# A transformer layer on one core: weight halves and matmul operands placed at chosen remainders of 128 bytes

## The chip, the cores and the metric

The kernel runs on one core of a Trainium2 chip. A core has a matrix engine (TensorE, PE in the rows; its weight loads are shown apart as PEld), a vector engine (VectorE, DVE), an activation engine (ScalarE, ACT), GpSimd (POOL) and a queue engine (SyncE, SP) that issues the transfers. The core's own memory has 128 partitions; a tile takes the same stretch of bytes in each of them, so that an address below is a byte offset within a partition. The metric is the device time of one execution in microseconds, median of several runs.

## The reference

One layer with 512 tokens and model width 2048, all in float32. Cut to what matters here:

```python
mod = silu(c) @ w_ada + b_ada                       # six vectors of 2048
h = rms_norm(x, norm1_g) * (1 + sc1) + sh1
proj = h @ w_in                                     # 2048 x 7168
o_hg = hgrn2_mixer(...)                             # 8 heads of gated recurrence
o_sb = stick_breaking_mixer(...)                    # 8 heads of causal attention
x = x + g1 * (concatenate([o_hg, o_sb]) @ w_out)    # 2048 x 2048
h = rms_norm(x, norm2_g) * (1 + sc2) + sh2
gate, up = split(h @ w_ffn_in)                      # 2048 x 11264
x = x + g2 * ((silu(gate) * up) @ w_ffn_out)        # 5632 x 2048
```

## The kernel before, in words

TensorE runs its big products at full rate in a reduced float32 format. To keep float32 accuracy each operand is split into a high half and a low half, and each product is three matmuls: high by high, high by low, low by high (`three`, `product`, `multiply`). The activations are split once and stay in memory (hhi and hlo, later ohi and olo, then opA to opD, then opsA to opsC). The weights are streamed: a transfer brings a tile into the ring "raw" (four buffers), `split` (L214) writes the high half with ScalarE (L220) and the low half with VectorE (L221) into the ring of three "hi" and three "lo" buffers of 4096 bytes, and TensorE reads those. From the input loop on, every fourth split goes to a pair of spare tiles instead: in the input loop hi2 and lo2 from the pool tp (`spare_here`, L1096), in the output half a part of the tile opsB (`spare_there`, from L1154).

The stages follow each other: the first projection (16 steps, accumulators st), eight heads of attention projection (sbp) with the attention of earlier heads between them, three projections per recurrence head (hgf, hgq, hgg) with the recurrence between them, the output projection (wo), a first gate tile (ff), the input loop of the feed-forward part (tiles f = 2 to 43; 7 products of 24 matmuls each, by a Strassen-like scheme, into ffA, ffB, ffC), and the output half (foA, foB, foC; 12 units of 7 products). VectorE also forms the rows of w_ada times c (L180) between them. The order of instructions is fixed when the program is built, by the code and by a planned clock in `Clock`; at run time each engine goes through its list in order.

In the first projection, in the attention projection and in the output half, a split weight tile is the moving operand and an activation tile the stationary one (in a row of a matmul, the names behind the arrow are the moving operand and then the stationary one). In the recurrence heads, the output projection and the input loop it is the other way round. Within a tile every slice that a matmul reads begins at a multiple of 512 bytes from the tile's start.

Where a tile starts is set by the pools. Left-hand pools stack from the low end in the order in which they are opened: const (cond, small, ones, epsb, lead, mod, gain1, gain2, rcol, ident2 and others), wp (raw, hi, lo), hp, and the stage's pools; a pool with side="right" stacks down from the top. Each tile is rounded up to 32 bytes. The small tiles of const (epsb of 4 bytes, lead of 8, rcol of 16) therefore set the remainder of everything behind them.

| tile | start before | remainder by 128 |
|---|---|---|
| ring raw | 11040 | 32 |
| ring hi (3 x 4096), ring lo | 43808, 56096 | 32 |
| hhi, ohi, opB, opsC | 68384 | 32 |
| hlo, olo, opC, opsB | 101152 | 32 |
| opA, opsA | 133920 | 32 |
| opD | 166688 | 32 |
| xo, x1, O | 196576 | 96 |
| spare hi2, lo2 of the input loop | 213984, 218080 | 96 |
| spare of the output half | within opsB | 32 |

Of the kernel before, what the change touches and what calls it, by code (L numbers as in the profile page):

```python
# [10 lines left out]
F32 = mybir.dt.float32  # L11
F32R = mybir.dt.float32r
# [5 lines left out]
P = 128  # L18
# [17 lines left out]
EPS = 1e-6  # L36
# [93 lines left out]
def trunk(ctx, tc, a):  # L130
    nc = tc.nc
    V, S, G = nc.vector, nc.scalar, nc.gpsimd
# [2 lines left out]

    const = ctx.enter_context(tc.tile_pool(name="const", bufs=1))
    wp = ctx.enter_context(tc.tile_pool(name="wp", bufs=3))
    xctx = ctx.enter_context(ExitStack())
    xop = xctx.enter_context(tc.tile_pool(name="xop", bufs=1, side="right"))
    hp = ctx.enter_context(tc.tile_pool(name="hp", bufs=1))  # L140
# [14 lines left out]
    ones = const.tile([P, P], F32, name="ones")  # L155
    G.memset(ones, 1.0)
    one = ones[:, 0:1]
    epsb = const.tile([P, 1], F32, name="epsb")
    G.memset(epsb, EPS)
    lead = const.tile([P, 2], F32, name="lead")  # L160
    left = [KT] * 6
    mod = const.tile([P, 96], F32, name="mod")
    gain1 = const.tile([P, KT], F32, name="gain1")
    gain2 = const.tile([P, KT], F32, name="gain2")
    rcol = const.tile([P, 4], F32, name="rcol")
    ident2 = const.tile([P, P], F32, name="ident2")

    def small_col(base, i=0):
        return small[:, base + i:base + i + 1]
# [9 lines left out]
    def gemv(w, row, col):  # L179
        V.scalar_tensor_tensor(w, w, 1.0, row, op0=ALU.mult, op1=ALU.mult, accum_out=col)  # L180

    def finish_gain(comp, k0, k1):
        g, base = (gain1, C_N1) if comp == SC1 else (gain2, C_N2)
        V.scalar_tensor_tensor(g[:, k0:k1], mod[:, comp * KT + k0:comp * KT + k1], 1.0, small[:, base + k0:base + k1],
                               op0=ALU.add, op1=ALU.mult)

    def ada(comp, k):
        j = comp * KT + k
        c = slice(j, j + 1)
        gemv(row_load(a["w_ada"][j], f"ada{j}"), cond, mod[:, c])  # L190
        left[comp] -= 1
        if comp == SC1:
            V.tensor_add(mod[:, c], mod[:, c], small_col(C_BADA, j))
            finish_gain(comp, k, k + 1)
        elif not left[comp]:
            all_k = slice(comp * KT, comp * KT + KT)
            V.tensor_add(mod[:, all_k], mod[:, all_k], small[:, C_BADA + comp * KT:C_BADA + comp * KT + KT])
            if comp == SC2:
                finish_gain(comp, 0, KT)
# [12 lines left out]
    def split(r, shape, name):  # L212
        count[0] += 1
        if spare and count[0] % 4 == 0:  # L214
            hi, lo = spare[0](shape, name)
        else:
            hi = wp.tile(shape, F32R, tag="hi", name=name + "h")
            lo = wp.tile(shape, F32R, tag="lo", name=name + "l")
        with tc.high_priority(offset=AHEAD):
            S.copy(hi, r)  # L220
            V.tensor_sub(lo, r, hi.bitcast(F32))  # L221
        return hi, lo

    def weights(src, shape, name):
        return split(load(src, shape, name), shape, name)
# [60 lines left out]
    for k in range(KT):  # L286
        xk = xo[:, k]
        if k == 0:
            for i in range(2):
                sl = slice(i * 1024, i * 1024 + 1024)  # L290
                gemv(r0[:, sl], cond[:, sl], lead[:, i:i + 1])
            j = SC1 * KT
            V.scalar_tensor_tensor(mod[:, j:j + 1], lead[:, 0:1], lead[:, 1:2], small_col(C_BADA, j), op0=ALU.add, op1=ALU.add)
            finish_gain(SC1, 0, 1)
            whi = wp.tile([P, 1024], F32R, tag="hi", name="wi0h")
            wlo = wp.tile([P, 1024], F32R, tag="lo", name="wi0l")
            for sl in (slice(0, T), slice(T, 2 * T)):
                S.copy(whi[:, sl], w0[:, sl])
                V.tensor_sub(wlo[:, sl], w0[:, sl], whi[:, sl].bitcast(F32))
        else:  # L300
            nc.sync.dma_start(xk, a["x"][:, k])
            ada(SC1, k)
            if k == 2:
                nc.sync.dma_start(cst, a["cst"])
            if k == KT - 1:
                nc.sync.dma_start(ident2, a["cst"][:, 0])
            whi, wlo = weights(a["w_hi"][k], [P, 1024], f"wi{k}")
        gk = gain1[:, k:k + 1]
        S.activation(hhi[:, k], xk, AF.Identity, scale=gk)
        V.scalar_tensor_tensor(hlo[:, k], xk, gk, hhi[:, k].bitcast(F32), op0=ALU.mult, op1=ALU.subtract)  # L310
        if k == 0:
            S.activation(ss1, xk, AF.Square)
        else:
            sq = sb.tile([P, T], F32, tag="qT" if k % 2 else "kT", name=f"sq{k}", bufs=1)
            S.activation(sq, xk, AF.Square)
            V.tensor_add(ss1, ss1, sq)
        for n in range(2):
            for t in range(4):
                ts_ = slice(t * P, t * P + P)
                cs = slice(n * T, n * T + T)  # L320
                out = banks[n * 4 + t]
                PE.matmul(out, hhi[:, k, ts_], whi[:, cs], start=(k == 0), stop=False)
                PE.matmul(out, hhi[:, k, ts_], wlo[:, cs], start=False, stop=False)
                PE.matmul(out, hlo[:, k, ts_], whi[:, cs], start=False, stop=(k == KT - 1))
# [12 lines left out]
    def sb_project(h):  # L337
        ps = [acc(f"sbp{h}_{t}") for t in range(4)]
        for c in range(8):
            if c % 2 == 0:  # L340
                raw = load(a["w_sb"][h, c // 2], [P, 2, 2, 384], f"wsb{h}_{c}")
            whi, wlo = split(raw[:, c % 2], [P, 2, 384], f"wsb{h}_{c}")
            pairs = [(kk, t) for kk in range(2) for t in range(4)]
            if c in (0, 7):
                pairs.sort(key=lambda p: p[1])
            for kk, t in pairs:
                k = 2 * c + kk
                ts_ = slice(t * P, t * P + P)
                out = ps[t][:, 0:384]
                PE.matmul(out, hhi[:, k, ts_], whi[:, kk], start=(k == 0), stop=False)  # L350
                PE.matmul(out, hhi[:, k, ts_], wlo[:, kk], start=False, stop=False)
                PE.matmul(out, hlo[:, k, ts_], whi[:, kk], start=False, stop=(k == KT - 1))
                clock.run()
        clock.until(lambda: h not in reuse or reuse[h] in done)
        if h in (0, 3):
            rows = scr[:, 0:3].rearrange("p a b -> p (a b)").rearrange("p (t c) -> p t c", t=4)
        else:
            rows = sb.tile([P, 4, 384], F32, tag="rows", name=f"rows{h}")
        for t in range(4):
            if t % 2:  # L360
                V.tensor_copy(rows[:, t], ps[t][:, 0:384])
            else:
                S.copy(rows[:, t], ps[t][:, 0:384])
        ready[h] = rows
# [234 lines left out]
    def mtile(src, name, xhi, xlo, out, nk=KT):  # L599
        n = 0  # L600
        raw = load(src, [P, nk, P], name)
        for c0 in range(0, nk, HALF):
            w = min(HALF, nk - c0)
            whi, wlo = split(raw[:, c0:c0 + w], [P, w, P], f"{name}_{c0}")
            for kk in range(w):
                three(out, whi[:, kk], wlo[:, kk], xhi[:, c0 + kk], xlo[:, c0 + kk], n == 0, n == nk - 1)
                n += 1
                clock.run()
# [734 lines left out]
```

## Time and profile before

| | |
|---|---|
| median of 3 runs | 2309.77 us (2309.41 to 2312.48) |
| the profiled execution's own time | 2309.45 us |
| its span, first to last instruction | 2307.6 us |
| mean granted TensorE clock | 0.995 of full |
| TensorE, VectorE, ScalarE busy | 2253.1, 1919.5, 1160.1 us |

The page gives busy times and their share of the span; a matmul's own duration there overlaps its neighbours', so the distance between the starts of two matmuls tells more than the duration of one. A window row gives, for a stretch in microseconds from the span's start, its length, the busy time of each engine with the number of instructions, the granted clock as a share of full, the transfers' share and their GB/s. A row of the chain of waits merges consecutive pieces of the same line and engine: start, length, what, and how many.

### The profile page before, as it was taken

How to read it: one execution, taken by the hardware profiler on the slowest of the kernel's cores; microseconds unless marked ns; L12 is line 12 of the kernel's file. 1: busy time of each engine (PE TensorE's matmuls, PEld its weight loads, DVE VectorE, ACT ScalarE, POOL GpSimd, SP SyncE). 2: the span in 40 equal slices, each digit the busy share in tenths (PEclk: the TensorE clock that was granted, in tenths of full speed). 3: DMA queues.
4: the chain of work that ended last, by engine and by line, in shares of the span. 5: the costliest groups of instructions: out<-in, count | busy, mean ns of one | idle time of the engine just before them, and what ended most of it. 6: DMA issues, size and time to landing. Idle time of an engine off the chain costs nothing.

```text
span 2307.6 us, 35720 instructions
## 1 busy us (share of the span) xinstructions
PE 2253.1 (98%) x14171; PEld 2049.8 (89%) x14171; DVE 1919.5 (83%) x2570; ACT 1160.1 (50%) x2011; POOL 10.7 (0%) x25
## 2 busy tenths in 40 slices
PE   8999899999999999989999999999999999999998
PEld 6899799888888788989999999999999978878776
DVE  8887779999887864699899988888888777888888
ACT  4326666565656422654445444454545545454443
POOL 0000000000000000000000000000000000000000
PEclk9999999999999999999999999999999999999999
DMA  9886446843322486336555534454544486654553
GB/s 368 314 319 225 166 153 230 305 170 126 110 92 76 155 294 209 111 114 238 206 203 197 209 133 165 142 174 142 174 142 157 177 343 237 219 178 142 183 204 87
DMA packets 114978, 437.69 MB, mean 190 GB/s; under 512 B 9822, under 2 KB 58236, under 8 KB 76796
## 3 DMA queue, kind: packets, MB, share of 16 engines
q1 hardware_dynamic: 114812, 435.42, 53.0%
q8 instruction: 111, 1.82, 0.3%
q14 instruction: 55, 0.45, 0.1%
HBM read 386.61 MB, written 48.77 MB: 189 GB/s over the span
## 4 chain that ended last, share of the span: by engine, by line
PE 79%; DVE 11%; DMA 4%; ACT 3%; issue 3%; SPq 0%; DVEq 0%; ACTq 0%
PE ffA L93 17%; PE ffC L93 9%; PE foA L93 8%; PE sbp L93 8%; PE wo L93 7%; PE ffB L93 4%; PE foC L93 4%; PE st L93 4%; PE hgf L93 4%; PE hgq L93 3%; PE hgg L93 3%; PE foB L93 1%; DVE ada L180 1%; PE l L93 1%; DMA opd<-fhi 1%
## 5 line engine op out<-in xcount | busy, mean ns | idle before, releaser
L180 DVE SCALAR_TENSOR_TENSOR ada<-ada,cond 128x2048 f32<-128x2048 f32 x95 | 216.9, 2286 | 49.0 <-DMA ada<-in_w_ada 49.0
L93 PE MATMUL ffA<-opD,ff_3h 128*128 128x256 f32 x512 | 93.6, 283 | 0.8 <-ACT u L1008 0.8
L93 PE MATMUL ffA<-opB,ff_6h 128*128 128x256 f32 x512 | 93.6, 283 | 0.2 <-ACT a L1008 0.2
L93 PE MATMUL ffC<-opB,ff_7h 128*128 128x256 f32 x512 | 93.5, 283 | 0.0
L93 PE MATMUL ffC<-opC,ff_4h 128*128 128x256 f32 x496 | 90.8, 284 | 0.4 <-ACT c L1008 0.3
L93 PE MATMUL ffB<-opA,ff_2h 128*128 128x256 f32 x496 | 91.3, 284 | 0.0
L93 PE MATMUL ffA<-opC,ff_5h 128*128 128x256 f32 x496 | 90.6, 283 | 0.0
L93 PE MATMUL ffA<-opA,ff_1h 128*128 128x256 f32 x496 | 90.6, 283 | 0.0
L1082 ACT CAST fhi<-forms 128x512 fp32r<-128x512 f32 (+1 forms) x63 | 43.6, 692 | 90.6 <-DMA opd<-fhi 74.1
L93 PEld LDWEIGHTS ffA<-opD,ff_3h 128*128 128x128 f32 x512 | 79.8, 192 | 1.0 <-ACT u L1008 1.0
L93 PEld LDWEIGHTS ffA<-opB,ff_6h 128*128 128x128 f32 x512 | 79.7, 192 | 0.4 <-ACT a L1008 0.4
L93 PEld LDWEIGHTS ffC<-opB,ff_7h 128*128 128x128 f32 x512 | 79.8, 192 | 0.0
L93 PEld LDWEIGHTS ffC<-opC,ff_4h 128*128 128x128 f32 x496 | 77.2, 192 | 0.8 <-ACT c L1008 0.8
L93 PEld LDWEIGHTS ffB<-opA,ff_2h 128*128 128x128 f32 x496 | 77.7, 193 | 0.1
L93 PEld LDWEIGHTS ffA<-opC,ff_5h 128*128 128x128 f32 x496 | 77.3, 192 | 0.0
L93 PEld LDWEIGHTS ffA<-opA,ff_1h 128*128 128x128 f32 x496 | 77.3, 192 | 0.0
L1083 DVE TENSOR_TENSOR forms<-forms,fhi 128x512 fp32r<-128x512 f32 (+1 forms) x63 | 49.0, 778 | 31.0 <-ACT fhi L1082 30.6
L93 PE MATMUL ffA<-opD,ff_3l 128*128 128x256 f32 x256 | 72.5, 283 | 0.0
L93 PE MATMUL ffC<-opB,ff_7l 128*128 128x256 f32 x256 | 72.4, 283 | 0.0
L93 PE MATMUL ffA<-opB,ff_6l 128*128 128x256 f32 x256 | 72.4, 283 | 0.0
L93 PE MATMUL ffB<-opA,ff_2l 128*128 128x256 f32 x248 | 70.3, 284 | 0.0
L93 PE MATMUL ffA<-opA,ff_1l 128*128 128x256 f32 x248 | 70.2, 283 | 0.0
(1644 smaller groups left out, 7759.3 us busy)
## 6 DMA issues: line engine op xcount, KB each, us to landing
ada<-in_w_ada SPq DMA_DIRECT2D x95, 1024.0 KB, 5.0
wfo<-in_w_fo SPq DMA_DIRECT2D x16, 1024.0 KB, 6.0
yraw<-in_w_fo SPq DMA_DIRECT2D x16, 1024.0 KB, 5.1
fix<-in_w_fix SPq DMA_DIRECT2D x14, 1024.0 KB, 5.7
opsA<-opd SPq DMA_DIRECT2D x12, 1024.0 KB, 4.9
opd<-forms SPq DMA_DIRECT2D x44, 256.0 KB, 3.7
opd<-fhi SPq DMA_DIRECT2D x42, 256.0 KB, 4.2
opd<-forms SPq DMA_DIRECT2D x22, 384.0 KB, 6.7
```

The source lines that it names most:

```text
L93: self.engine.matmul(out, lhsT, rhs, **kw)
L180: V.scalar_tensor_tensor(w, w, 1.0, row, op0=ALU.mult, op1=ALU.mult, accum_out=col)
L1082: S.copy(hi, R[:, q])
L1083: V.tensor_sub(R[:, q].bitcast(F32R), R[:, q], hi.bitcast(F32))
```

## The change

The small tiles whose sizes set the remainders are taken out of const: epsb becomes the first column of epsw (24 columns, 96 bytes) in a new pool edge at the very top, which shifts all right-hand tiles by 96 bytes; lead becomes 64 bytes in a pool ahead of the ring; rcol becomes 64 bytes in a pool behind it; and the ring of hi and lo halves moves from wp to a pool wq of its own between the two, with as many buffers as before.

```diff
     wp = ctx.enter_context(tc.tile_pool(name="wp", bufs=3))
+    ahead = ctx.enter_context(tc.tile_pool(name="ahead", bufs=1))
+    wq = ctx.enter_context(tc.tile_pool(name="wq", bufs=3))
+    behind = ctx.enter_context(tc.tile_pool(name="behind", bufs=1))
+    edge = ctx.enter_context(tc.tile_pool(name="edge", bufs=1, side="right"))
...
-    epsb = const.tile([P, 1], F32, name="epsb")
-    G.memset(epsb, EPS)
-    lead = const.tile([P, 2], F32, name="lead")
+    epsw = edge.tile([P, 24], F32, name="epsw")
+    G.memset(epsw, EPS)
+    epsb = epsw[:, 0:1]
+    lead = ahead.tile([P, 16], F32, name="lead")
...
-    rcol = const.tile([P, 4], F32, name="rcol")
+    rcol = behind.tile([P, 16], F32, name="rcol")
...
-            hi = wp.tile(shape, F32R, tag="hi", name=name + "h")
-            lo = wp.tile(shape, F32R, tag="lo", name=name + "l")
+            hi = wq.tile(shape, F32R, tag="hi", name=name + "h")
+            lo = wq.tile(shape, F32R, tag="lo", name=name + "l")
...
-            whi = wp.tile([P, 1024], F32R, tag="hi", name="wi0h")
-            wlo = wp.tile([P, 1024], F32R, tag="lo", name="wi0l")
+            whi = wq.tile([P, 1024], F32R, tag="hi", name="wi0h")
+            wlo = wq.tile([P, 1024], F32R, tag="lo", name="wi0l")
```

| tile | start after | remainder by 128 |
|---|---|---|
| ring raw | 10944 | 64 |
| ring hi, ring lo | 43776, 56064 | 0 |
| hhi, hlo, opA, opD and what follows in their places | 68416, 101184, 133952, 166720 | 64 |
| xo, x1, O | 196480 | 0 |
| spare hi2, lo2 of the input loop | 213888, 217984 | 0 |
| spare of the output half | within opsB | 64 |

The sequence of instructions on every engine is the same as before, with the same waits; the only difference is the name epsw for epsb and the width of the one instruction of GpSimd that sets it.

## Rows read from the trace of the kernel before

**Rows 1.** The page, busy time of each engine.
```profile
PE 2253.1 (98%) x14171; PEld 2049.8 (89%) x14171; DVE 1919.5 (83%) x2570; ACT 1160.1 (50%) x2011; POOL 10.7 (0%) x25
```

**Rows 2.** Busy time by window, cut at the stages; the first line names the columns.
```profile
core 0: us, PE busy (x) PEld busy (x) DVE busy (x) ACT busy (x) POOL busy (x), PEclk, DMA share, GB/s
11.50:101.50 90.00, 89.96 (x385) 74.09 (x386) 80.49 (x116) 38.66 (x52) 0.00 (x0) 1.00 0.95 356
101.50:257.00 155.50, 146.71 (x822) 141.84 (x821) 125.10 (x152) 64.13 (x112) 0.00 (x0) 0.98 0.72 262
257.00:437.80 180.80, 178.97 (x1075) 169.97 (x1074) 150.33 (x221) 114.31 (x320) 0.00 (x0) 0.99 0.55 196
437.80:767.00 329.20, 327.70 (x1675) 275.26 (x1673) 287.94 (x541) 200.32 (x442) 9.05 (x16) 1.00 0.36 131
767.00:954.00 187.00, 183.44 (x865) 152.18 (x866) 116.49 (x147) 59.89 (x95) 0.00 (x0) 1.00 0.60 210
954.00:1008.20 54.20, 47.61 (x388) 46.74 (x387) 54.20 (x139) 45.21 (x106) 0.00 (x0) 0.99 0.32 110
1008.20:1312.50 304.30, 301.83 (x2520) 301.18 (x2521) 281.41 (x318) 150.76 (x221) 0.00 (x0) 0.99 0.57 203
1312.50:1850.30 537.80, 537.36 (x4538) 536.96 (x4537) 441.02 (x500) 268.66 (x391) 0.00 (x0) 1.00 0.46 159
1850.30:2307.60 457.30, 439.56 (x1914) 351.57 (x1912) 378.86 (x432) 211.99 (x269) 0.00 (x0) 0.99 0.56 197
```

**Rows 3.** The chain of waits at two products: start us, length us, what, count.
```profile
1216.21 2.88 PE ffB L93 x24
1219.09 2.72 PE ffA L93 x24
```

**Rows 4.** TensorE's timeline there: start us, length us, line, output<-operands, columns, count.
```profile
1218.57 0.40 PE L93 MATMUL ffB<-opA,ff_2h 128*128 128x256 f32 x2
1218.81 0.28 PE L93 MATMUL ffB<-opA,ff_2l 128*128 128x256 f32 x1
1218.93 0.39 PE L93 MATMUL ffA<-opB,ff_6hi 128*128 128x256 f32 x2
1219.15 0.28 PE L93 MATMUL ffA<-opB,ff_6lo 128*128 128x256 f32 x1
```

**Rows 5.** The chain of waits, unbroken runs of wider matmuls in three stages.
```profile
57.86 42.16 PE st L93 x186
...
392.08 8.32 PE sbp L93 x48
...
810.91 130.51 PE wo L93 x574
```

**Rows 6.** TensorE's timeline at two float32 products of the attention.
```profile
237.45 0.81 PE L93 MATMUL zA<-kT,qT 128*128 128x384 f32 x2
238.09 1.45 PE L93 MATMUL zB<-kT,qT 128*128 128x256 f32 x4
```

**Rows 7.** VectorE's groups by shape: count, busy us, mean ns, idle before.
```profile
L221 DVE TENSOR_TENSOR wfo_2l<-wfo,wfo_2h 128x1024 fp32r<-128x1024 f32 x32 | 39.1, 1222 | 11.5 <-ACT wfo_2h L220 11.3
L221 DVE TENSOR_TENSOR ff_5l<-ffS,ff_5h 128x1024 fp32r<-128x1024 f32 x31 | 37.8, 1219 | 0.0
```

**Rows 8.** The chain of waits between 100 and 260 us, VectorE's part.
```profile
119.72 4.54 DVE xo L498 x8
...
206.04 4.83 DVE fix L180 x5
```

**Rows 9.** TensorE's waits, 101.5 to 257 and 1850 to 2308 us: total, times, longest.
```profile
PE tB L98 <- ACT I L450: 3.2, 1, 3.2
PE sbp L93 <- DVE wsb_0l L221: 1.8, 1, 1.8
...
PE foC L93 <- DVE wfo_2l L221: 2.7, 5, 0.5
```

**Rows 10.** VectorE's longest wait, 1008 to 1312 us.
```profile
DVE ada L180 <- DMA ada<-in_w_ada: 7.1, 9, 1.7
```

## The prediction

> **What bounds the kernel now.** I read the busy times first: TensorE is busy 98% of the span, the next engine 83% [rows 1]. That alone says little, so I cut the span into nine stretches at the borders of the stages [rows 2]. In eight of the nine TensorE is busy over 94% of the stretch. The granted clock is 0.98 to 1.00 of the upper level, 2.4 GHz, in all of them, so clock time is not what can be won. The exception is 954 to 1008 us, where VectorE is busy for all 54.20 us and TensorE for 47.61. So the question is how far apart two matmuls stand when nothing is waited for, since a busy engine may still be a slow one.
>
> For that I used the chain of waits, where an unbroken run of matmuls is one row with a count. In the feed-forward input loop 24 matmuls take 2.88 us, 120.0 ns each; but 24 others, of the same shape, take 2.72 us, 113.3 ns each [rows 3]. The timeline of those instants names them: the first read their weight halves from the ring (ff_2h, ff_2l), the second from the two spare tiles (ff_6hi, ff_6lo) [rows 4]. Shape and order within a product are alike, and both moving operands start at the same remainder. What differs is the weights' place: before the change the ring starts 32 bytes past a multiple of 128, as do all operand tiles (opA to opD), and the spare tiles start 96 bytes past one, that is 64 bytes away from the operands. The reader is to see 2.72 against 2.88 and nothing else in those rows.
>
> Next, whether the wider matmuls carry the same surplus. 256 columns at 2.4 GHz are 106.7 ns, so the ring's matmuls lose 13.3 ns and the spare tiles' 6.7. With 384 columns, 48 matmuls in 8.32 us are 173.3 ns against 160: 13.3 lost. With 512 columns, 186 in 42.16 us are 226.7 ns and 574 in 130.51 us are 227.4, against 213.3: 13.3 to 14.1 lost [rows 5]. In all of these both operands start 32 bytes past a multiple of 128. The loss is a fixed amount per matmul, whatever its width, and only where the operands are 64 bytes apart is half of it gone. One more row bounds it: float32 matmuls of the attention, both operands again at 32, run two records of 384 columns in 0.64 us (237.45 to 238.09), 320 ns each, which is two cycles a column with no surplus [rows 6]. So the loss belongs to full-rate streams.
>
> **The change part by part.** Nothing is added to or taken from any engine's list and no wait is new; what moves is where tiles start. (1) The ring goes to 0 past a multiple of 128, hhi, hlo, opA to opD and the later operand tiles to 64, the spare tiles of the input loop to 0. I count from the loops the full-rate matmuls whose two operands were at the same remainder and now are 64 bytes apart: 384 in the first projection, 1536 in the attention projection (eight heads), 1152 in the recurrence heads, 816 in the output projection, 384 in the first gate tile, 5280 in the input loop (three quarters of 42 x 168), 1344 in the output half. That is 10,896. (2) The 1776 matmuls on spare tiles in the input loop stay 64 bytes apart: 0. (3) The output half's own spare tiles lie inside an operand tile, so they move with it: 504 matmuls stay at the same remainder: 0. (4) epsw is set in 24 columns instead of 1, by GpSimd, before the first matmul at 11.5 us, on an engine busy 10.7 us in all [rows 1]: 0. lead and rcol only grow; their extra columns are unused: 0. (5) VectorE and ScalarE read the moved tiles too. Subtractions that form a low half take 1219 ns with inputs at 96 and 32 and 1222 ns with both at 32 [rows 7], so I cost this at 0; no row has an input at 0 or 64, and 0.5% of VectorE's time in the stretches where it is late would be about 3 us either way.
>
> The price of (1) per matmul: the row with the same spacing of operands gives 6.67 ns. For 384 and 512 columns, and with the roles exchanged (ring tile moving, operand tile stationary), the trace has no row at 64 apart; the bounds are 0 and the whole 13.3 ns. I take 6.67 there too, because the loss is the same at three widths. In all 10,896 x 6.67 ns = 72.6 us off TensorE's list. How much of it reaches the end is read stretch by stretch [rows 2]:
>
> First projection and attention heads 0 to 3, 7.7 us: TensorE waits here for VectorE's and ScalarE's chain, with VectorE's updates of xo and its fix reductions on the chain [rows 8] and waits of 3.2 and 1.8 us [rows 9]. A faster matmul arrives earlier and waits longer; I keep 1.0. Attention heads 4 to 7, 5.1 us: 1.8 us of 180.8 is idle, but every head hands TensorE's results to ScalarE and back; I keep 3.0. Recurrence heads, 7.7 us: TensorE 327.7 of 329.2, VectorE 287.9; I keep 6.5. Output projection, 5.4 us: 130.51 us of it run without a wait; I keep 4.5. First gate tile, 2.6 us: VectorE has no gap, 0. Input loop, tiles 2 to 16, 12.6 us: VectorE is busy 281.4 of 304.3 and waits 7.1 more for rows of w_ada [rows 10], so shortened to 291.7 it would have 3 us left; I keep 8.5. Tiles 17 to 43, 22.6 us: VectorE 441 of 537.8, afterwards of 515; I keep 22.5. Output half, 9.0 us: VectorE 378.9 of 457.3, and some of its halves already arrive last [rows 9]; I keep 5.0. Sum 51.0 us. The profiled execution took 2309.45 us, 1.85 more than its span; 2309.45 - 51.0 = 2258.5, and the median of the runs lies 0.3 above that execution: 2259 us.
>
> A rule against it: the Trainium skill, "SBUF — State Buffer", section "SBUF: two separate sides", says that TensorE reads moving operand and weights through two ports of its own and never waits on anyone. By it the operands' distance could not matter, and this change would be worth 0; the trace does show two spacings [rows 3], but not which property of the place makes them. What hangs on that rule is the third rival.
>
> **The rivals.** First, more than half of the loss goes. All tiles were 32 bytes off a multiple of 64 and now none of the big ones is; the surplus of 6.7 ns that the spare tiles still have may come from that, and the half-rate rows show that a matmul can run with none [rows 6]. Against it: those rows are at 32 too. Then up to 145 us leave the ring's matmuls and 11.8 the spare ones, and VectorE becomes the bound in the input loop: tiles 2 to 16 cannot fall below 281.4 + 7.1, a gain of 15.8; tiles 17 to 43 fall to 27 x 168 x 106.7 ns = 484 us plus some waits, a gain of 45; the other stretches give 34. Together 95: 2215 us. The Trainium skill, "TensorE: Matmul & The Clock Gate", section "Wait — 56ns, not 53.3ns?", gives bf16 matmuls a floor of N / 2.4 GHz + 2.5 ns; by that figure, an estimate, the full loss would not quite go, and the time would be some 15 us above this rival's; no full-rate run here shows such a spacing.
>
> Second, the matmuls do get faster, but VectorE and ScalarE hold the rest back everywhere except in tiles 17 to 43, where VectorE has a fifth of its time free. Then 22.5 and 2 or 3 elsewhere remain: 2285 us.
>
> Third, no change: the short spacing belongs to the spare tiles for another reason, say that they lie in the upper half of the memory (from 213984 on, the ring below 68384). They stay there, the ring stays below: 2309 us.
>
> Fourth, slower: it is the weight tile's own start that counts, 96 past a multiple of 128 being a good one and 32, 0 and 64 not. Nothing separates this from the distance in [rows 3, 4]. No weight tile lies at 96 any more, so the 1776 spare matmuls go from 113.3 to 120.0 ns: 11.8 us, all in the input loop where TensorE sets the pace: 2321 us. It decides as soon as the spare products take 2.88 us.
>
> **How the numbers follow.** Forecast (2240 to 2280) 0.48; first rival (2210 to 2240) 0.25; second (2280 to 2302) 0.10; third 0.07; fourth 0.10. I tell changes over 0.2%, 4.6 us, from none: faster 0.83, same 0.07, slower 0.10. The range 2210 to 2302 holds the first three cases but for their tails.
>
> **What would show it.** In the chain of the changed kernel, ring products of 24 matmuls take 2.72 us like the spare ones, 384 columns run at 166.7 ns and 512 at 220.0: the price is right. 2.60 us or less speaks for the first rival, 2.88 everywhere for the fourth. If the price is right and the time is not, the stretches tell where it stayed: tiles 17 to 43 should shrink from 537.8 to about 515, tiles 2 to 16 from 304.3 to about 296, and 954 to 1008 should stay at 54. The forecast is wrong if the wide matmuls keep 227 ns while the 256-column ones gain, or if VectorE's own operations change by more than 1%.

## The result, and the profile after

The changed kernel takes 2319.69 us (median of 5 runs, 2314.27 to 2322.26), the kernel before in the same comparison 2311.02 us. The ratio is 1.0033, with a 95% interval of 1.0021 to 1.0046: slower, where 51 us less had been forecast. The profiled execution of the changed kernel took 2321.66 us, with a span of 2319.8.

The page's line of busy times answers to [rows 1].

```profile
PE 2249.7 (97%) x14171; PEld 2026.6 (87%) x14171; DVE 1917.5 (83%) x2570; ACT 1154.2 (50%) x2011; POOL 10.7 (0%) x25
```

TensorE is busy 3.4 us less, VectorE and ScalarE as much as before to within 6 us, and yet the span grew by 12.2 us. The windows, cut at the changed kernel's own stage borders, answer to [rows 2]; the columns are the same.

```profile
11.70:103.90 92.20, 92.17 (x385) 73.97 (x386) 80.71 (x116) 38.48 (x52) 0.00 (x0) 1.00 0.92 348
103.90:441.10 337.20, 327.38 (x1895) 313.24 (x1894) 275.73 (x373) 178.45 (x431) 0.00 (x0) 0.98 0.63 226
441.10:772.70 331.60, 329.51 (x1676) 275.70 (x1674) 288.90 (x541) 201.35 (x444) 9.03 (x16) 1.00 0.36 131
772.70:961.30 188.60, 186.01 (x865) 153.02 (x866) 115.32 (x147) 58.64 (x93) 0.00 (x0) 0.99 0.59 209
961.30:1015.50 54.20, 46.86 (x388) 45.84 (x386) 54.20 (x140) 45.20 (x106) 0.00 (x0) 0.98 0.32 110
1015.50:1857.00 841.50, 820.24 (x7057) 813.61 (x7058) 719.96 (x817) 414.39 (x613) 0.00 (x0) 0.99 0.50 175
1857.00:2319.80 462.80, 447.54 (x1913) 351.16 (x1911) 379.05 (x432) 211.55 (x269) 0.00 (x0) 0.99 0.55 195
```

Set beside the lengths of [rows 2] (windows of one stage added together; the border between recurrence and output projection before is put at 767.9 us, where the first matmul of the output projection starts, as after; [rows 2] have it at 767.0):

| stage | before, us | after, us | difference | forecast |
|---|---|---|---|---|
| first projection | 90.0 | 92.2 | +2.2 | -1.0, with heads 0 to 3 |
| attention projection | 336.3 | 337.2 | +0.9 | -3.0, heads 4 to 7 |
| recurrence | 330.1 | 331.6 | +1.5 | -6.5 |
| output projection | 186.1 | 188.6 | +2.5 | -4.5 |
| first gate tile | 54.2 | 54.2 | 0 | 0 |
| input loop | 842.1 | 841.5 | -0.6 | -31.0 |
| output half | 457.3 | 462.8 | +5.5 | -5.0 |
| sum | | | +12.0 | -51.0 |

Two things went otherwise than forecast: every stage with wide matmuls grew, and the input loop, which was to give 31 us, gave nothing. The loop's window shows what kind of miss that is: before, TensorE was busy 839.2 of 842.1 us in it (301.83 + 537.36, [rows 2]), now 820.24 of 841.5. Its matmuls became shorter, and it stands idle for 21 us. The granted clock has a small part in the sum: the trace of the changed kernel has two spells of 3.4 us at the lower level (1.2 GHz) that the kernel before had not, one at the start of the output projection and one in the loop. At half the rate each costs at most 1.7 us.

The chain of waits shows the spacings, as [rows 3, 5] did. First two pieces of the wide stages, then one of the loop, then the first product of the output half:

```profile
395.12 8.39 PE sbp L93 x48
...
817.30 131.79 PE wo L93 x574
...
1034.56 5.44 PE ffA L93 x48
...
1862.64 5.56 PE foA L93 x24
```

The first product of the output half in the kernel before:

```profile
1855.96 5.44 PE foA L93 x24
```

The products of the loop shown take 5.44 us for 48, 113.3 ns each, where ring products took 120.0: the price of the one row known beforehand was right. Not all reach it. Of the 6760 distances from start to start within the loop's products 5191 are 115 ns or less and 1478 are 116 to 119; the 24 matmuls behind the wait shown below stand 118 ns apart. The 574 matmuls of the output projection take 131.79 us (229.6 ns), 130.51 before; 48 of 384 columns 8.39 (174.8 ns), 8.32 before. The output half's first product of 24 takes 5.56 us (231.7 ns), 5.44 (226.7 ns) before. None of these wide rows gained, and all lost.

Where the loop's idle time comes from, the chain shows around 1070 us, from a transfer to a late product:

```profile
1070.69 6.42 DMA opd<-fhi
...
1077.19 0.63 ACT fhi L1087
...
1077.83 2.19 DMA opd<-fhi
...
1080.11 0.63 ACT fhi L1087
1080.73 0.94 ACT ff_5h L225
1081.67 0.28 ACT a L1013
...
1081.99 3.09 PE ffA L93 x24
```

fhi is the one buffer in which `parts` (L1082 before, L1087 after) puts the high half of the loop's results before three stores per pair of tiles carry it to memory. The next cast into it waits until the store of the last one has landed. ScalarE works in order, so behind that waiting cast stand the split ff_5h and the copy `a`, a tap (L1013) that reads an accumulator out, and behind the copy stands TensorE, which waits for that accumulator. TensorE's waits for such taps (u and b are two of them), from 1015 to 1857 us in the changed kernel (total, times, longest):

```profile
PE ffA L93 <- ACT u L1013: 7.9, 6, 2.4
PE ffA L93 <- ACT b L1013: 7.8, 10, 1.4
```

In the loop of the kernel before, u stands with 2.2 us, and b not at all. The page's line of costliest groups for the cast into fhi, in the kernel before and then in the changed one (before the bar the busy time and the mean, behind it the idle time ahead of it and what ended most of that):

```profile
L1082 ACT CAST fhi<-forms 128x512 fp32r<-128x512 f32 (+1 forms) x63 | 43.6, 692 | 90.6 <-DMA opd<-fhi 74.1
```

```profile
L1087 ACT CAST fhi<-forms 128x512 fp32r<-128x512 f32 (+1 forms) x63 | 43.7, 694 | 141.5 <-DMA opd<-fhi 104.6
```

The wait was there before, with 74.1 us, when TensorE was busy for 839.2 of the loop's 842.1 us; the run before_fhi below shows how little it cost there. In the changed kernel a tile of the loop that nothing disturbs takes 168 x 113.3 ns = 19.04 us, but in most of the loop its period alternates between 19.0 to 19.5 and 20 to 21 us.

### The profile page after: what moved, and what is told of

It reads as the page before. It is cut to its first block, busy times and chain, and to the rows that moved or that the text cites. A ratio compares the mean times of both kernels' runs of the same rounds, so it can differ in the third digit from the quotient of the medians.

```text
span 2319.8 us, 35720 instructions
## 1 busy us (share of the span) xinstructions
PE 2249.7 (97%) x14171; PEld 2026.6 (87%) x14171; DVE 1917.5 (83%) x2570; ACT 1154.2 (50%) x2011; POOL 10.7 (0%) x25
## 4 chain that ended last, share of the span: by engine, by line
PE 65%; DVE 17%; DMA 9%; issue 5%; ACT 4%; SPq 0%; DVEq 0%; ACTq 0%
PE ffA L93 10%; PE foA L93 9%; PE sbp L93 7%; PE wo L93 7%; PE ffC L93 5%; PE foC L93 4%; PE st L93 4%; PE hgf L93 4%; DMA opd<-fhi 3%; PE hgq L93 3%; PE hgg L93 3%; PE ffB L93 3%; PE foB L93 1%; PE l L93 1%; DVE ada L185 1%
## 5 line engine op out<-in xcount | busy, mean ns | idle before, releaser
L1087 ACT CAST fhi<-forms 128x512 fp32r<-128x512 f32 (+1 forms) x63 | 43.7, 694 | 141.5 <-DMA opd<-fhi 104.6
L93 PE MATMUL ffC<-opB,ff_7h 128*128 128x256 f32 x512 | 88.7, 276 | 0.0
L93 PE MATMUL ffC<-opC,ff_4l 128*128 128x256 f32 x248 | 68.8, 278 | 0.0
```

Of the source, the lines that this page charges most:

```text
L93: self.engine.matmul(out, lhsT, rhs, **kw)
L1087: S.copy(hi, R[:, q])
```

## The experiments

The theory after the comparison: first, full-rate matmuls of 384 and 512 columns get slower, not faster, when their operands leave the place relative to each other that they had; second, the loop's gain is eaten by ScalarE's wait for the one store buffer. The rivals: the wide stages suffer from something else in the change, and the loop is held by VectorE or by splits as such.

**sweep: the disputed price by itself.** Not the layer: bursts of 48 matmuls with nothing else running, at 256 (p), 384 (q) and 512 (r) columns, the moving and the stationary operand 0, 32, 64 or 96 bytes (A to D, in this order; first the moving one) past the same remainder by 512.

```diff
+    for w, letter in WIDTHS:
+        for m, mn in enumerate(REM):
+            for s, sn in enumerate(REM):
+                ps = psum.tile([P, T], F32, tag="ps", name=f"{letter}{mn}{sn}")[:, 0:w]
+                for n in range(48):
+                    mo = 8 * m + (n % 8) * T
+                    so = 8 * s + (n % 32) * P
+                    PE.matmul(ps, sta[:, so:so + P], mov[:, mo:mo + w], start=(n == 0), stop=(n == 47))
```

> This kernel is not the layer: it writes a block of x to the output, and runs 48 bursts of 48 full-rate matmuls without a wait: widths 256 (p), 384 (q) and 512 (r), moving operand (first letter) and stationary operand (second letter) each at 0 (A), 32 (B), 64 (C) or 96 (D) bytes past a multiple of 128. Theory 1 (the loss depends on the distance of the two operands and on the width): 256 columns 120 ns at the same remainder and 113.3 at 64 apart, for every pair with that distance; 384 columns 173.3 and about 175; 512 columns 226.7 at the same remainder, 229 where the moving one is 64 and the stationary one 0, 233 the other way round. Theory 2 (the stationary tile's own start counts): columns of the table alike whatever the moving remainder. Theory 3 (alignment of either to 64 counts): pairs AA, AC, CA, CC alike and different from BB, BD, DB, DD.

The chain gives a row per burst: start, us for 48, name.

```profile
33.53 5.75 PE pAA L48 x48
...
84.58 5.61 PE pCB L48 x48
...
124.43 8.32 PE qAA L48 x48
...
149.46 8.48 PE qAD L48 x48
...
258.53 10.93 PE rAA L48 x48
...
280.65 11.20 PE rAC L48 x48
...
347.56 11.00 PE rCA L48 x48
...
425.23 10.88 PE rDD L48 x48
```

Equal letters, that is operands at the same place, take 5.75 us at 256 columns, 8.32 to 8.35 at 384 and 10.88 to 10.93 at 512, whatever the letter: the start itself doesn't matter. Apart, 256 columns gain (5.61 to 5.68, but one of 5.76), 384 take 8.32 to 8.48 and 512 lose, 10.99 to 11.23. So the sign changes with the width, in bursts that hold nothing else of the layer. The gain at 256 columns is only 1.5 to 3 ns here, against 6.7 in most of the loop; why the loop's is larger isn't settled.

**after_fhi: the store buffer alone.** The changed kernel with a second buffer.

```diff
-                hi = tp.tile([P, b - a, HT], F32R, tag="fhi", name=f"fhi{f}_{a}", bufs=1)
+                hi = tp.tile([P, b - a, HT], F32R, tag="fhi", name=f"fhi{f}_{a}", bufs=2)
```

> The changed kernel with two buffers instead of one for fhi, the high half that is stored to memory in the input loop. Theory 1 (in the input loop the faster matmuls now wait for ScalarE, and ScalarE, in order, for the store of the one fhi buffer): the input loop, 841.5 us in the changed kernel and 799.7 by its 7056 matmuls at 113.3 ns, falls to 805 to 815, most of it in tiles 17 to 43, and the time to 2285 to 2295. Theory 2 (VectorE or the loads of the next weights bound the loop): less than 8 us of change, 2312 or more.

Measured: 2294.13 us, ratio to the kernel before 0.9936 (0.9921 to 0.9951). The window of the input loop, and ScalarE's wait in it (total, times, longest):

```profile
1016.50:1830.80 814.30, 810.03 (x7057) 808.46 (x7058) 721.16 (x817) 420.93 (x613) 0.00 (x0) 0.99 0.50 181
```

```profile
ACT fhi L1087 <- DMA opd<-fhi: 28.7, 21, 4.8
```

The loop went from 841.5 to 814.3 us, with VectorE's busy time in it unchanged (719.96 and 721.16), and ScalarE's wait for the store fell from 104.6 to 28.7. It was the store, and neither VectorE nor the splits; the 27.2 us are most of the 31.0 that had been forecast for the loop.

**narrow: only the 256-column products apart.** The kernel before with longer ring buffers, meant to put the wide products' operands at one place again.

```diff
+    def ring(tag, shape, name, far):
+        n = int(np.prod(shape[1:]))
+        t = wp.tile([P, 1056], F32R, tag=tag, name=name)[:, 16 * far:16 * far + n]
...
-    def split(r, shape, name):
+    def split(r, shape, name, far=0):
...
-            hi = wp.tile(shape, F32R, tag="hi", name=name + "h")
-            lo = wp.tile(shape, F32R, tag="lo", name=name + "l")
+            hi, lo = ring("hi", shape, name + "h", far), ring("lo", shape, name + "l", far)
...
-        return split(raw, [P, HALF, P], name)
+        return split(raw, [P, HALF, P], name, 1)
```

> The kernel before, its ring buffers 128 bytes longer; the 256-column products (first gate tile, input loop, last output tile) read ring tiles from 64 bytes in, so that all of them are 64 apart from their operand; all wider products keep both operands at the same remainder. Theory 1 (the change lost its time in the 384 and 512 columns): first projection 90, attention 336, recurrence 330, output projection 186, output half 453 us as before; 24-matmul products of the input loop at 2.72; the loop about 841 as in the changed kernel; in all within 3 us of the kernel before, some 10 us under the changed one. Theory 2 (the wide stages lost by something else than the operands' distance, the new places of other tiles): they stay at the changed kernel's lengths only if that is still there, so they return here too, but then the sweep shows no width dependence.

Measured: 2316.4 us, ratio 1.0025 (1.0015 to 1.0035). The wide stages didn't come back; the chain of the output projection:

```profile
818.07 133.63 PE wo L93 x574
```

232.8 ns each, the slowest so far, with both operands at the same remainder by 128. But the buffers are 4224 bytes long, 33 x 128, so that of neighbouring ring buffers every other one now starts 128 bytes further within 256. The rule "same remainder by 128" was mine, and it is wrong, as sweep_far shows below.

**narrow_fhi: the same with two store buffers.**

> The kernel narrow with two fhi buffers. Theory 1 (width decides, and the one fhi buffer bounds the input loop): both gains add, wide stages as before and the input loop at 805 to 815: 2309 - 30 = about 2280 us, 0.987 of before. Theory 2 (VectorE or the loads bound the loop): within 8 us of before.

Its edit is that of after_fhi. Measured: 2296.03 us, ratio 0.9939 (0.9922 to 0.9955), the loop 818.7 us. The second buffer brings some 20 us here as well; for the wide stages it has the fault of narrow.

**sweep_far: how far the distance counts.** The bursts again, with one operand 0 to 448 bytes off in steps of 64 (A to H); m: the moving operand is the one shifted, s: the stationary one. The stationary slices go round after 28 instead of 32.

```diff
-        for m, mn in enumerate(REM):
-            for s, sn in enumerate(REM):
+        for d, dn in enumerate(DIST):
+            for way in "ms":
...
+                dm, ds = (16 * d, 0) if way == "m" else (0, 16 * d)
```

> Not the layer: 48 bursts of 48 full-rate matmuls; widths 256, 384, 512 columns (first letter p, q, r of an accumulator's name), the two operands 0 to 448 bytes apart in steps of 64 (second letter A to H), by moving either the moving operand (m) or the stationary one (s). Theory (what counts is moving minus stationary start, modulo 512 bytes; sizes from the runs so far): 256 columns: A 5.75 us per 48 (119.8 ns), B to H 5.4 to 5.65; 384: A 8.32, distance 64 8.32, 128 and 384 8.5, 448 8.4; 512: A 10.9, Bm (64) 11.0, Dm..Fm near 256 11.0, C and G (128, 384) 11.15, Hm (448) 11.2; and each m burst equals the s burst of the opposite letter (Bm = Hs, Cm = Gs). Rival 1 (only the remainder by 128 counts): C, E and G equal A at every width: 5.75, 8.32, 10.9. Rival 2 (the operand's own start counts, not the distance): m and s bursts differ in a way that the opposite letters do not mirror.

```profile
33.48 5.75 PE pAm L49 x48
...
50.64 5.46 PE pBs L49 x48
...
78.79 5.75 PE pEm L49 x48
...
140.73 8.32 PE qBm L49 x48
149.05 8.47 PE qBs L49 x48
...
191.22 8.34 PE qEm L49 x48
...
258.37 10.92 PE rAm L49 x48
...
280.16 11.01 PE rBm L49 x48
291.17 11.19 PE rBs L49 x48
302.37 11.15 PE rCm L49 x48
...
335.90 11.00 PE rDs L49 x48
346.90 10.90 PE rEm L49 x48
```

E, 256 bytes apart, equals A at every width (5.75, 8.34, 10.90), while C, 128 apart, does not (11.15). So neither 128 nor 512, which I had expected, is the period, but 256: at every width F, G and H repeat B, C and D to 0.01 us. At 384 and 512 columns it is moving start minus stationary start that counts: 64 ahead takes 11.01 as Bm and 11.00 as Ds (minus 192), 64 behind 11.19 as Bs and 11.20 as Dm. At 256 columns this mirror fails: 64 behind takes 5.46 as Bs, but 5.65 as Dm, and 5.66 in sweep with the same two starts as Bs (pAC). At 384 columns that pair of starts also differs between the two runs, 8.39 against 8.47. So something besides the distance has a part below 512 columns. Per matmul, these rows divided by 48, beside the median distance from one start to the next in the layer (128 from narrow, the others from the kernel before and the changed one):

| moving minus stationary, modulo 256 | 256 columns, ns | 384 | 512 |
|---|---|---|---|
| 0: bursts / layer | 120 / 120 | 173 / 173 | 227 / 227 |
| 64 | 118 / 113, first gate tile 118 | 173 / none | 229 / 229 |
| 128 | 119 / none | 176 / 176 | 232 to 233 / 233 |
| 192 | 114 to 118 / 113 | 176 / 174 | 233 / 233 |

A distance from start to start belongs to two matmuls: in narrow, 0 and 128 take turns, and the 574 matmuls of the output projection average 232.8 ns, above any mix of 227 and 232 to 233 with a good part at 0. The table doesn't explain that. At 256 columns the first gate tile and the loop of the changed kernel have one distance, 64, and 118 and 113 ns.

The kernel before had 0 everywhere but for the loop's spare tiles: the best place for wide matmuls (at 384 columns 64 is as good) and the worst of the table for those of 256 columns.

**before_fhi: the second buffer without the change.** The edit of after_fhi, in the kernel before.

> The kernel before with one edit: the store buffer fhi of the input loop has two buffers instead of one. No tile that TensorE reads moves. Theory (the store's landing bounds the input loop only once its matmuls are 113 ns apart): the loop of 842.3 us is held by 5280 matmuls at 120 ns and 1776 at 113.3 (834.8 us), so at most 7 us are to be had: 2303 to 2308, ratio 0.997 to 1.000. Rival (the second buffer is worth its 25 us wherever it is put): loop about 815 us, total about 2284, ratio 0.989.

Measured: 2307.8 us, ratio 0.9985 (0.9976 to 0.9995), the loop:

```profile
1007.40:1846.20 838.80, 838.51 (x7057) 838.16 (x7058) 722.91 (x817) 421.42 (x613) 0.00 (x0) 1.00 0.50 176
```

3.3 us of the loop (842.1 to 838.8), not 25: with matmuls at 120 ns TensorE is the bound there, busy 838.51 of 838.80. The same buffer is worth five to eight times as much once most stand at 113.3 (17.6 us between the next two runs, 27.2 in the changed kernel).

**same512: the loop's operands alone moved.** The kernel before, with opA to opD 64 bytes further, the loop's spare tiles shifted too, and the output half's operands put back to the ring's place.

```diff
+    def moved(pool, tag, name, h, n, at=16):
+        t = pool.tile([P, h * 4096 + n], F32R, tag=tag, name=name)[:, at:at + h * 4096]
+        return t.rearrange("p (a j i t) -> p a j i t", a=h, j=HALF, i=2)
...
-    early = fh.tile([P, 2, HALF, 2, HT], F32R, tag="b1", name="opA")
+    early = moved(fh, "b1", "opA", 2, 112, 0)
...
-    later = hp.tile([P, 2, HALF, 2, HT], F32R, tag="hlo", name="opC")
+    later = moved(hp, "hlo", "opC", 2, 16)
```

> The kernel before, with the operand tiles of the feed-forward input loop alone moved: opA to opD start 64 bytes past the ring's remainder by 512, the spare tiles 64 bytes past those; every other operand pair (st, sbp, hg, wo, fo) stays at the same remainder by 512, as before. fhi has one buffer. Theory: wide stages as before (st 90, attention projection 336, recurrence 330, output projection 186, output half 453 us); the loop's matmuls at 113.3 ns, but the loop held by the fhi store, 836 to 842 us: total 2303 to 2310, ratio 0.997 to 1.000. Rival (the wide stages were slowed by something else in the change than distance, or gain by themselves): they stay at the changed kernel's 92, 337, 332, 189, 459. Rival (loop not held by the store): loop 815 us, total 2283.

Measured: 2306.88 us, ratio 0.9988 (0.9977 to 0.9999). The output projection's run, and the loop:

```profile
813.31 130.51 PE wo L93 x574
```

```profile
1010.50:1847.00 836.50, 818.67 (x7057) 812.33 (x7058) 719.78 (x817) 414.50 (x614) 0.00 (x0) 1.00 0.50 176
```

The 574 matmuls take 130.51 us again, to the hundredth what they took in [rows 5]: moving the loop's operands alone costs them nothing. Of the other wide stages the first projection (89.8 us), the attention projection (336.6) and the output half (456.9) are where they were, but the recurrence has 330.9 us, between 330.1 before and 331.6 after. This kernel holds nothing else of the change, so it can't show by itself that nothing else slowed the wide stages. That it was the distance rests on the bursts, which with nothing else running have 229.4 and 233.1 ns at 512 columns (Bm and Bs), where the changed kernel has 229.6 in the output projection (distance 64) and a mean of 233.3 in the first projection (distance 192). The loop stands idle for 18 us, as after the change.

**best: both together.** same512 with two store buffers.

> The kernel of the run same512 with two fhi buffers. Theory (both causes together): wide stages as in the kernel before (st 90, attention projection 336, recurrence 330, output projection 186, output half 453 us), first gate tile 54, loop about 814: total 2280 to 2284, ratio 0.987 to 0.989. Rival (the second buffer's gain is the same 25 us but the slower wide stages come from elsewhere): 2294, ratio 0.993, as with the changed kernel and two buffers.

Measured: 2287.79 us (4 runs, 2283.28 to 2288.72), ratio 0.9895 (0.9878 to 0.9911), faster than both kernels. Its windows, in the order of the table above:

```profile
12.00:101.20 89.20, 89.20 (x385) 73.52 (x386) 80.39 (x116) 38.79 (x52) 0.00 (x0) 1.00 0.95 359
101.20:437.80 336.60, 325.58 (x1895) 311.32 (x1894) 275.57 (x373) 178.52 (x431) 0.00 (x0) 0.98 0.62 226
437.80:769.00 331.20, 328.37 (x1676) 275.27 (x1674) 289.03 (x541) 201.29 (x444) 9.05 (x16) 1.00 0.37 131
769.00:957.90 188.90, 186.35 (x865) 154.23 (x866) 115.53 (x147) 59.18 (x93) 0.00 (x0) 0.98 0.59 208
957.90:1012.00 54.10, 46.79 (x388) 45.92 (x386) 54.10 (x139) 45.16 (x106) 0.00 (x0) 0.98 0.32 110
1012.00:1830.90 818.90, 809.38 (x7057) 806.38 (x7058) 720.86 (x817) 420.43 (x613) 0.00 (x0) 1.00 0.50 180
1830.90:2286.30 455.40, 437.75 (x1912) 350.25 (x1911) 378.69 (x432) 211.92 (x269) 0.00 (x0) 1.00 0.56 198
```

First projection, attention projection and output half are back at the lengths of [rows 2], to 0.3 us, or below. The total is 4 to 8 us longer than expected; three stages are longer than in the kernel before or, for the loop, than in after_fhi. The output projection has 188.9 instead of 186.1, and the granted clock is 0.98 there, where it was 1.00: the trace has one spell of 6.8 us at the lower level (1.2 GHz) at its beginning, which the kernel before had not. At half the rate that costs at most 3.4 us, which can cover the difference. The loop has 818.9 where after_fhi had 814.3: TensorE waits 5.4 us in it for the tap b, against 0.4 in after_fhi; why that tap comes late no run shows. The recurrence has 331.2 where 330.1 stood, and for that I have no cause that a run shows.

## Why the prediction was wrong

*"The loss is a fixed amount per matmul, whatever its width"* and *"I take 6.67 there too, because the loss is the same at three widths."* This step failed first. The trace had one row with operands apart, at 256 columns. The equal surplus of 13.3 ns at three widths was true, but it is the surplus at distance 0 only; what another distance gives depends on the width. The bounds "0 and the whole 13.3 ns" left out a loss without a reason that excluded it. By the layer's means over distances under 240 ns (512 columns: 227.5 ns before, 229.3 at 64, 233.3 at 192; 384 columns: 173.7 before, 174.8 at 192) the change costs 1872 x 1.8 + 1728 x 5.8 + 1536 x 1.1 = 15.1 us of TensorE's list outside the loop (1872: recurrence and output projection without its last tile, whose 96 matmuls have 256 columns; 1728: first projection and output half; 1536: attention projection), where the prediction took off 34.9 and let 20.0 reach the end. The windows show +12.6 there, of which the lower clock at the start of the output projection may be up to 1.7.

*"Tiles 17 to 43, 22.6 us: VectorE 441 of 537.8, afterwards of 515; I keep 22.5"*, and 8.5 for tiles 2 to 16. This step failed second. The sum looked for what is late next by busy shares, and asked VectorE alone; ScalarE, at about half its time busy, seemed free. But a wait holds an engine that works in order as busy work does, and the page already listed 74.1 us of waits for the store of fhi. The loop gave 0.6 of the 31.0 us; 27.2 more came with the second buffer.

*The 256-column price* was right for most of the loop's 5280 ring matmuls, which fell from 120.0 to 113.3 ns; some stayed at 118, and so did most of the first gate tile, which the sum rightly gave no share in the end. *The first gate tile* at 54.2 us was right. *VectorE's operations at no cost* was right to within the noise: 719.96 us in the loop, where 722.4 (281.41 + 441.02, [rows 2]) stood.

The rivals: the first fell, since the rows of the changed kernel have no product below 113.3 ns. The second was right that something other than TensorE would hold the time, ScalarE among them, but it kept the 22.5 us of tiles 17 to 43, the greater part of what was then lost. The third fell with the ring's 113.3 ns. The fourth gave 2321 us, next to the measured time, and is wrong all the same: it decides when spare products take 2.88 us, and in the changed kernel seven products in a row, spare ones among them, take 2.72 each. The time is the sum of two other things.

A section of the Trainium skill was weighed there: "SBUF — State Buffer", "SBUF: two separate sides", by which TensorE never waits for anyone. The measurement decides against taking this to mean that an operand's place is free: with no other engine at work, 48 matmuls of 512 columns take 10.9 us with their two operands at distance 0 and 11.2 with the stationary one 64 bytes further.

What stays open: why the distance counts, and why with opposite signs at 256 and 512 columns; what besides the distance decides between 113 and 118 ns at 256 columns; why the wide matmuls of narrow are slower than the table gives; and the late tap in the loop of best. No run has the whole change with the operands back at distance 0.

## What to carry to other kernels

A price read at one shape holds for that shape: before it is extended to others, let its range reach to a loss, or measure a burst of each shape by itself, which takes a kernel of one page. When the busiest engine is made faster, list the in-order waits of every engine in that stage, also of those half idle, and what stands behind them; a buffer with one copy that a store must leave first is a clock of its own. Two changes can each be worth nearly nothing alone (0.9985 and 0.9988 here) and 1% together (0.9895).

## What the runs showed of the hardware

In these runs the spacing of full-rate matmuls repeats when one operand is moved by 256 bytes, and moving both alike changes nothing. At 384 and 512 columns it follows the distance of the moving operand's start from the stationary one's, modulo 256. At 512 columns 0 is best (226.7 ns) and 192 the worst of the steps of 64 (233.3); at 384, 0 and 64 are best (173.3), and 128 and 192 cost 1 to 3 ns. At 256, 0 is worst of the steps of 64 (119.8), and other distances have 113 to 119, more than one value at the same distance. The stores from fhi took 6.42 and 2.19 us from issue to landing in the chain shown, beside casts of 0.63 us.
